# A hybrid decoder layer on one core: 512-column output projection, spread tables, shared gate-weight buffers, division on ScalarE, odd quarters' low parts on VectorE

## The chip, the cores and the metric

The kernel runs on one core of one Trainium2 chip. A core has TensorE (PE, the matrix unit), VectorE (DVE), ScalarE (ACT), GpSimd (POOL) and SyncE (SP), which here issues the DMAs. Each engine works through its own list of instructions in order and waits on semaphores for the others. The metric is the device time of one execution in microseconds (us); lower is better.

## The reference

The input is x (2048 positions by 1024) and 256 memory rows. All is float32.

```python
hn = _rmsnorm(h, norm_g[l])
proj = hn @ w_in[l]
(a_in, a_gate, c_in, c_b, c_c, c_gate, q, q_gate) = jnp.split(proj, split_idx, axis=-1)
y_ssm = _s5_group(a_in, ...) * jax.nn.silu(a_gate)
y_conv = _short_conv_group(c_in, c_b, c_c, conv_w[l], conv_b[l]) * jax.nn.silu(c_gate)
y_mem = _memory_xattn_group(q, mem_n, w_mem_kv[l]) * jax.nn.silu(q_gate)
```

The widths are 384 for each of the six state-space and convolution parts and 256 for q and its gate. The state-space group (`_s5_group`) is a scan over positions, a GELU, and a sigmoid gate with a 384 by 384 weight `w_glu`. The memory group is a softmax attention of four heads over the 256 memory rows. The three outputs are concatenated (1024 wide), multiplied by `w_out` (1024 by 1024), added to the residual x, and normalised once more.

## The kernel before

**Tiling.** The 2048 positions are worked in four quarters of 512 (q = 0 to 3). Every float32 product is made of three TensorE matmuls (`mm3`, L79 to L83): each operand is split into a rounded "high" part and the rest, the "low" part, and high times high, high times low and low times high are added up in PSUM. `split` (L85) makes the high part by a copy on ScalarE (L86) and the low part by a subtraction on VectorE or GpSimd (L77).

**Weights.** `wtile` (L127) loads 512 KB of weights into a staging buffer (two of them for most weights), splits it, and keeps both parts in one of three shared buffers (tag "wl"). Its argument `e` is the engine of the low part: in `proj` that is VectorE for quarter 0 and GpSimd for quarters 1 to 3. An odd quarter has 22 such tiles (3 for a_in, 2 for q, 2 for its gate, 3 for the a-gate, 12 for the convolution). The weights of the output projection (`wout`, tag names wo) have eight tiles per quarter, each 512 rows by 256 columns. The GLU's weights (`wg`) have three tiles of 128 columns with buffers of their own ("wg"), staged in a buffer that the loads of the scan's outputs (`gr`) use too.

**Stages.** In order of time: a prologue with the first rows and the projection of a_in for quarter 0; the gate and attention projections of quarter 0 with the building of four tables of the scan (`gen_table`) woven in at a fixed rate by `interleave`; the convolution of quarter 0, keys and values of the memory; then for quarters 1 and 3 the projections (`main`, all of 512 columns) together with the scan over two quarters (`ssm`, tiles W, sC, ps_y, ps_v), the GLU (`glu`, psg) and the attention (`attention`: scores sps, exponential pe, transposes trp, product po); quarter 2 with less beside it; and after each a stage of output projection (`outproj`, matmuls of 256 columns into PSUM tiles po). The last stage is `outproj(3)` with the GLU of quarter 2 woven in, then `outproj_last(2)`.

**What sets the order.** The Tile framework schedules the program with its own timeline and writes a fixed list for each engine, so a change in one part can move instructions elsewhere. PSUM banks and buffers are reused in a ring: a matmul into a new tile waits until the reader of the tile that held the bank before has finished. `gate2` (L619: ua, uq, uc) is such a reader: it frees the bank of a projection.

**The division.** In `attention` the 128 by 256 pieces of exponentials are divided by their sums on VectorE (L785); 64 such instructions in all.

Of the kernel before, what the change touches and what calls it, by code (L numbers as in the profile page):

```python
# [15 lines left out]
P = 128  # L16
# [29 lines left out]
def hymba_layer_kernel(  # L46
# [29 lines left out]
    def tt(o, a, b, op, e=V):  # L76
        e.tensor_tensor(o, a, b, op)  # L77
# [22 lines left out]
    def sumsq(xt, ss, junk):  # L100
        S.activation(junk, xt, AF.Square, accum_out=ss)
# [586 lines left out]
    def merge(a, b, rate):  # L688

# [70 lines left out]
    def attention(q, j):  # L760
# [52 lines left out]
    def glu(q):  # L813
# [13 lines left out]
            split(y_ssm[:, 0, t], y_ssm[:, 1, t], gr)  # L827
            yield
        for m in range(3):
            w = wtile(w_glu[0, :, m * P:(m + 1) * P], WS, P, f"wg{q}{m}", V, late["wg"], "a")  # L830
            ps = ps_ss.tile([P, QL], F32, tag="ss", name=f"psg{q}{m}")
            for k in range(3):
                mm3(ps, w[:, 0, k, :], w[:, 1, k, :], y_ssm[:, 0, k, :], y_ssm[:, 1, k, :], k == 0, k == 2)
            t_, g2 = (swk.tile([P, QL], F32, tag="pg", bufs=2, name=f"gt{q}{m}{z}") for z in range(2))
            S.activation(t_, ps, AF.Tanh, bias=bg[:, m:m + 1], scale=0.25)
            tt(g2, f32(y_ssm[:, 0, m, :]), f32(y_ssm[:, 1, m, :]), ALU.add, G)
            V.scalar_tensor_tensor(g2, t_, 1.0, g2, ALU.add, ALU.mult)
            V.scalar_tensor_tensor(us[m], g2, 0.125, us[m], ALU.mult, ALU.mult)
            yield
# [2 lines left out]
        yield  # L842


    yk = [("ssm", 0), ("ssm", 1), ("ssm", 2), ("conv", 0), ("conv", 1), ("mem", 0), ("mem", 1), ("conv", 2)]
    rows = [0, 1, 2, 3, 4, 6, 7, 5]

    def fetch_y(q):

# [16 lines left out]
    def omm(q, ps, i, kh, w, first):  # L866

        o_ = slice(i * P, (i + 1) * P)
        for k in range(4):
            nm, kk = yk[4 * kh + k]  # L870
            kr = rows[4 * kh + k] - 4 * kh
            mm3(ps, Y[q][nm][:, 0, kk, o_], Y[q][nm][:, 1, kk, o_], w[:, 0, kr, :], w[:, 1, kr, :],
                first and k == 0, kh == 1 and k == 3, skip_group_check=True)

    def residual(q, last=False):

# [9 lines left out]
                nc.sync.dma_start(h[z][u * NCH:(u + 1) * NCH], xq[q, u][:, 2 * z:2 * z + 2])  # L886
        return h

    def wout(q, n_, kh, dst=None, st="w", e=G):
        src = w_out[0, kh * 512:(kh + 1) * 512, n_ * 256:(n_ + 1) * 256]  # L890
        return wtile(src, 512, 256, f"wo{q}{n_}{kh}", e, dst, st)

    def outproj(q):
        h = residual(q)
        for n_ in range(4):
            ns = slice(n_ * 256, (n_ + 1) * 256)
            pss = [ps_mm.tile([P, 2, 256], F32, tag="mm", name=f"po{q}{n_}{b}") for b in range(2)]
            for kh in range(2):
                w = wout(q, n_, kh)
                for i in range(4):  # L900
                    omm(q, pss[i // 2][:, i % 2, :], i, kh, w, kh == 0 and i % 2 == 0)
                    yield
            for b in range(2):
                hb = h[b][:, :, ns]
                tt(hb, pss[b], hb, ALU.add)
# [15 lines left out]
    def outproj_last(q):  # L921
# [14 lines left out]
        ws = [[wout(q, n_, kh, dsts[2 * n_ + kh], "wx"[kh], V if kh else G) for kh in range(2)] for n_ in range(4)]  # L936
# [11 lines left out]
        for n_ in range(4):  # L948
            ns = slice(n_ * 256, (n_ + 1) * 256)
            ps = ps_mm.tile([P, 2, 256], F32, tag="mm", name=f"po{q}{n_}")  # L950
            for kh in range(2):
                for i in range(2):
                    omm(q, ps[:, i, :], i, kh, ws[n_][kh], kh == 0 and i == 0)
            for i in range(2):
                tt(h[i][:, ns], ps[:, i], h[i][:, ns], ALU.add)
                sumsq(h[i][:, ns], ss[:, i, n_:n_ + 1], junk[0][:, 0:256])
        for i in range(2):
            V.scalar_tensor_tensor(h[i], h[i], rstd(i, 4), fg_b, ALU.mult, ALU.mult)
            store(i, h[i])
        for i in range(2, 4):  # L960
            parts = [(0, 1), (2, 3)] if i == 2 else [(0, 1), (2,), (3,)]
            for b, ns_ in enumerate(parts):
                ns = slice(ns_[0] * 256, ns_[-1] * 256 + 256)
                ps = ps_mm.tile([P, 2, 256], F32, tag="mm", name=f"po{q}{i}_{b}")
                for a, n_ in enumerate(ns_):
                    for kh in range(2):
                        omm(q, ps[:, a, :], i, kh, ws[n_][kh], kh == 0 and a == 0)
                pv = ps.rearrange("p a n -> p (a n)")[:, :256 * len(ns_)]
                tt(h[i][:, ns], pv, h[i][:, ns], ALU.add)
                sumsq(h[i][:, ns], ss[:, i, b:b + 1], junk[1][:, :256 * len(ns_)])  # L970
# [35 lines left out]
    kv = memory_kv()  # L1006
# [49 lines left out]
```

## Time and profile before

| | before |
|---|---|
| median of three runs | 902.94 us (900.92 to 909.04) |
| the profiled execution | 904.45 us |
| its span from first to last instruction | 902.5 us |
| PE busy | 843.1 us (93%) |
| PEld (loading of weights into the array, beside PE) | 723.7 us (80%) |
| DVE busy | 613.7 us (68%) |
| ACT busy | 367.0 us (41%) |
| POOL busy | 301.7 us (33%) |
| mean granted TensorE clock | 0.975 |

A busy share counts instructions that overlap only once; TensorE's matmuls are pipelined, so the duration of one is longer than the distance to the next. Idle time of an engine is shown with what released it. "Granted clock" is the share of TensorE's full clock that the chip allowed in a stretch.

### The profile page before, as it was taken

The numbers are of one execution on the slowest core, as the hardware profiler recorded it, in microseconds if no ns is written. First come the engines' busy times: TensorE is split into PE (matmuls) and PEld (weight loads), VectorE is DVE, ScalarE is ACT, GpSimd is POOL, SyncE is SP. The second block draws the span as 40 slices with busy tenths as digits, with TensorE's granted clock in tenths as the row PEclk, the third lists the DMA queues.
The fourth block names the chain that finished last, engine by engine and source line by source line (L and its number), as shares of the span: only waits on it lengthen the run. The fifth ranks groups of instructions, "written<-read, shape, count | busy, mean of one in ns | idle before, by whom it ended". The sixth has DMA issues, their size and how long they took to land. (4 is left out here: it accounts for less than half of the span.)

```text
span 902.5 us, 13173 instructions
## 1 busy us (share of the span) xinstructions
PE 843.1 (93%) x4876; PEld 723.7 (80%) x4876; DVE 613.7 (68%) x1244; ACT 367.0 (41%) x706; POOL 301.7 (33%) x157
## 2 busy tenths in 40 slices
PE   2998999889998998999999899999999998989996
PEld 2985777778877877899888688899878876879996
DVE  6898899583998896936434664344399996865353
ACT  5343433545343434433444533335233344444511
POOL 2000001154222344444545434334443343455400
PEclk9999899999997999999999999999999999999999
DMA  9553649966464534454575632656757744493362
GB/s 205 161 150 103 189 131 269 267 187 201 125 179 130 156 93 119 108 152 141 159 239 150 160 114 84 161 165 186 214 156 207 211 128 125 117 222 112 125 177 57
DMA packets 180647, 142.97 MB, mean 158 GB/s; under 512 B 41192, under 2 KB 164584, under 8 KB 180584
## 3 DMA queue, kind: packets, MB, share of 16 engines
q1 hardware_dynamic: 180584, 142.14, 56.4%
q8 instruction: 38, 0.62, 0.3%
q14 instruction: 25, 0.20, 0.1%
HBM read 113.80 MB, written 26.74 MB: 156 GB/s over the span
## 5 line engine op out<-in xcount | busy, mean ns | idle before, releaser
L77 POOL TENSOR_TENSOR wo<-wo_st,wo 128x1024 fp32r<-128x1024 f32 x26 | 63.8, 2454 | 70.6 <-ACT wo L86 59.2
L77 DVE TENSOR_TENSOR h<-po,h 128x512 f32<-128x512 f32 (+1 forms) x37 | 22.2, 615 | 43.5 <-PE po L83 34.5
L81 PE MATMUL po<-wo,yssm 128*128 128x256 f32 x168 | 48.5, 289 | 1.8 <-ACT yssm L86 1.8
L83 PE MATMUL po<-wo,yssm 128*128 128x256 f32 x168 | 48.2, 287 | 0.0
L82 PE MATMUL po<-wo,yssm 128*128 128x256 f32 x168 | 47.8, 285 | 0.0
L780 ACT ACTIVATE pe<-sps,nm 128x256 f32<-128x256 f32 x64 | 29.5, 472 | 39.4 <-DVE nm L778 35.1
L81 PE MATMUL psai<-hn,wai 128*128 128x512 f32 (+1 forms) x120 | 42.7, 362 | 2.8 <-ACT hn L86 2.1
L82 PE MATMUL psai<-hn,wai 128*128 128x512 f32 (+1 forms) x120 | 42.5, 356 | 0.3 <-DVE hn L77 0.2
L83 PE MATMUL psai<-hn,wai 128*128 128x512 f32 (+1 forms) x120 | 42.0, 353 | 0.0
L81 PE MATMUL pscg<-hn,wcg 128*128 128x512 f32 x96 | 39.8, 415 | 2.2 <-ACT wcg L86 2.2
L86 ACT CAST wo<-wo_st 128x1024 fp32r<-128x1024 f32 x27 | 28.2, 1044 | 33.3 <-PE po L83 16.2
L81 PE MATMUL po<-wo,yconv 128*128 128x256 f32 x144 | 40.7, 283 | 0.0
L83 PE MATMUL po<-wo,yconv 128*128 128x256 f32 x144 | 40.3, 280 | 0.0
L82 PE MATMUL po<-wo,yconv 128*128 128x256 f32 x144 | 40.1, 279 | 0.0
L83 PE MATMUL pscg<-hn,wcg 128*128 128x512 f32 x96 | 39.1, 407 | 0.5 <-DVE wcg L77 0.5
L81 PE MATMUL psag<-hn,wag 128*128 128x512 f32 x96 | 39.5, 411 | 0.0
L82 PE MATMUL pscg<-hn,wcg 128*128 128x512 f32 x96 | 39.0, 407 | 0.0
L77 POOL TENSOR_TENSOR wcb<-wcb_st,wcb 128x1024 fp32r<-128x1024 f32 x9 | 22.9, 2550 | 47.9 <-ACT wcb L86 47.9
L83 PE MATMUL psag<-hn,wag 128*128 128x512 f32 x96 | 38.5, 401 | 0.0
L82 PE MATMUL psag<-hn,wag 128*128 128x512 f32 x96 | 38.4, 400 | 0.0
L81 PE MATMUL pscb<-hn,wcb 128*128 128x512 f32 x96 | 38.3, 399 | 0.0
L81 PE MATMUL psci<-hn,wci 128*128 128x512 f32 x96 | 38.3, 399 | 0.0
(710 smaller groups left out, 2903.5 us busy)
## 6 DMA issues: line engine op xcount, KB each, us to landing
wo_st<-in_w_out_dram SPq DMA_DIRECT2D x32, 512.0 KB, 3.8
tb<-t_dram SPq DMA_DIRECT2D x16, 960.0 KB, 5.5
out_dram<-h SPq DMA_DIRECT2D x32, 256.0 KB, 3.4
h<-in_x_dram SPq DMA_DIRECT2D x14, 512.0 KB, 7.4
wai_st<-in_w_in_dram SPq DMA_DIRECT2D x12, 512.0 KB, 4.3
wag_st<-in_w_in_dram SPq DMA_DIRECT2D x12, 512.0 KB, 4.3
wci_st<-in_w_in_dram SPq DMA_DIRECT2D x12, 512.0 KB, 4.2
wcc_st<-in_w_in_dram SPq DMA_DIRECT2D x12, 512.0 KB, 4.1
```

What stands on the lines that cost most here:

```text
L77: e.tensor_tensor(o, a, b, op)
L81: T.matmul(ps, lh, rh, start=first, stop=False, **kw)
L82: T.matmul(ps, lh, rl, start=False, stop=False, **kw)
L83: T.matmul(ps, ll, rh, start=False, stop=last, **kw)
L86: S.copy(hi, src)
L780: S.activation(pe[:, a, h], sps[h][:, a], AF.Exp, bias=nm_[:, a, h:h + 1], accum_out=sm[:, a, h:h + 1])
```

## The change

Five things are edited. (1) The output projection uses matmuls of 512 columns: a tile of weights is now 256 rows by 512 columns, and four PSUM banks (three "mm", one "po") are filled over four pairs of row blocks. Only the last 512 columns of the last 128 rows are done as two matmul groups of 256, so 1,488 of the 1,536 matmuls of 256 columns become 744 of 512 and 48 stay. (2) The tables of the scan are woven in at a lower rate and over a longer stretch, up to the keys and values of the memory. (3) The GLU's weights are two tiles (256 and 128 columns) in the shared "wl" and "ws" buffers. (4) The division by the softmax's sums moves from VectorE to ScalarE. (5) The low parts of the projections' weights for quarters 1 and 3 move from GpSimd to VectorE.

```diff
     def proj(q, c0, nm):
-        w = wtile(w_in[0, :, c0:c0 + P], DM, P, f"w{nm}{q}", G if q else V)
+        w = wtile(w_in[0, :, c0:c0 + P], DM, P, f"w{nm}{q}", G if q == 2 else V)
...
+    def weave(main, side, rate):
+        acc = 0.0
+        for _ in main:
+            acc += rate
+            while acc >= 1.0:
+                acc -= 1.0
+                next(side, None)
+            yield
...
             for a in range(2):
                 for h in range(2):
-                    V.tensor_scalar(pe[:, a, h], pe[:, a, h], sm[:, a, h:h + 1], None, ALU.mult)
+                    S.activation(pe[:, a, h], pe[:, a, h], AF.Copy, scale=sm[:, a, h:h + 1])
...
         for m in range(3):
-            w = wtile(w_glu[0, :, m * P:(m + 1) * P], WS, P, f"wg{q}{m}", V, late["wg"], "a")
+            if m % 2 == 0:
+                c1 = min(m * P + 256, WS)
+                wg = wtile(w_glu[0, :, m * P:c1], WS, c1 - m * P, f"wg{q}{m}", V)
+            w = wg[:, :, :, m % 2 * P:m % 2 * P + P]
...
+    def omm(q, ps, i, kp, w, cs=slice(0, 512)):
         o_ = slice(i * P, (i + 1) * P)
+        for k in range(2):
+            nm, kk = yk[2 * kp + k]
+            mm3(ps, Y[q][nm][:, 0, kk, o_], Y[q][nm][:, 1, kk, o_], w[:, 0, k, cs], w[:, 1, k, cs],
+                kp == pairs[0] and k == 0, kp == pairs[-1] and k == 1)
...
+    def wout(q, nh, kp, dst=None, st="w", e=G):
+        src = w_out[0, kp * 256:(kp + 1) * 256, nh * 512:(nh + 1) * 512]
+        return wtile(src, 256, 512, f"wo{q}{nh}{kp}", e, dst, st)
...
-        for n_ in range(4):
-            ns = slice(n_ * 256, (n_ + 1) * 256)
-            pss = [ps_mm.tile([P, 2, 256], F32, tag="mm", name=f"po{q}{n_}{b}") for b in range(2)]
-            for kh in range(2):
-                w = wout(q, n_, kh)
+        for nh in range(2):
+            ns = slice(nh * 512, (nh + 1) * 512)
+            pss = [ps_mm.tile([P, 512], F32, tag="mm", name=f"po{q}{nh}{b}") for b in range(3)]
+            pss.append(ps_po.tile([P, QL], F32, tag="po", name=f"po{q}{nh}3"))
+            for kp in pairs:
+                w = wout(q, nh, kp)
                 for i in range(4):
-                    omm(q, pss[i // 2][:, i % 2, :], i, kh, w, kh == 0 and i % 2 == 0)
+                    omm(q, pss[i], i, kp, w)
                     yield
...
-    interleave(chain(agate(0), qproj(0), conv(0, 0), conv(0, 1)), chain(mem_rows(), gens), 2.2)
+    side = chain(mem_rows(), gens)
+    for _ in weave(chain(agate(0), qproj(0), conv(0, 0), conv(0, 1)), side, 1.5):
+        pass
+    interleave(weave(merge(conv(0, 2), memory_kv(), 0.7), side, 0.9), prep(1), 2.0, 4)
+    for _ in side:
+        pass
     open_left()
-    interleave(merge(conv(0, 2), kv, 0.7), prep(1), 2.0, 4)
```

The first place is VectorE in the fourth block of the first scan (about 272 to 279 us before). sC is the scan's state that the ps_y matmuls read; uq (L619) is the reader that frees the PSUM bank which the third a-gate projection of quarter 1 (psag) takes next. Before, from the one to the other:

```order
482 L77 TENSOR_TENSOR sC_2799<-W_2793,m203w 128x3x128
483 L809 SCALAR_TENSOR_TENSOR uq_1190<-pe_2124,uq_1190 128x512
484 L539 COPY st_2421<-sC_2799 128x3
485 L523 STREAM_SHUFFLE m_2906<-ps_v_2810 128x384
486 L77 TENSOR_TENSOR m_2906<-m_2906,tb_2808 128x384
487 L535 COPY sC_3017<-st_137 128x3
488 L77 TENSOR_TENSOR m_2905<-ps_v_2810,tb_2808 128x384
489 L77 TENSOR_TENSOR m_2905<-m_2905,m_2906 128x384
490 L619 SCALAR_TENSOR_TENSOR uq_2633<-thq_2631,psqg_2606 128x512
```

In the changed kernel sC_2796 is row 488, and these are the last twelve rows to the same uq; the eight rows between are two score maxima, parts of the attention's output and the first steps of the next scan block:

```order
497 L552 SCALAR_TENSOR_TENSOR m103g<-m103g,ps_y_2854 128x384
498 L77 TENSOR_TENSOR m_2903<-m_2903,tb_2805 128x384
499 L77 TENSOR_TENSOR m_2902<-m_2902,m_2903 128x384
500 L792 RECIPROCAL sm_2503<-sm_2503 128x4
501 L530 SCALAR_TENSOR_TENSOR W_2908<-rho,st_138,m_2902 128x128 x3
502 L788 TENSOR_REDUCE nm_2646<-sps_2632 128x2
503 L554 SCALAR_TENSOR_TENSOR ge_2862<-m103g,ps_y_2854 128x384
504 L533 STREAM_SHUFFLE m204w<-W_2908 128x384
505 L788 TENSOR_REDUCE nm_2646<-sps_2633 128x2
506 L77 TENSOR_TENSOR W_2908<-W_2908,tb_2805 128x384
507 L77 TENSOR_TENSOR m204w<-m204w,tb_2805 128x384
508 L619 SCALAR_TENSOR_TENSOR uq_2630<-thq_2628,psqg_2603 128x512
```

The reader moved from 8 rows behind sC to 20 rows behind it.

The second place is ScalarE at the start of the stage of `outproj(3)`. thc is the last step on the last projection of quarter 3, hy are high parts of quarter 2's outputs, wo are output weights, wg the GLU's weights. Before:

```order
458 L617 ACTIVATE thc_7300<-pscg_7275 128x512
459 L86 CAST hy_7307<-fy_7308 128x512 x2
460 L86 CAST hy_7307<-fy_7314 128x512 x2
461 L86 CAST hy_7307<-fy_7320 128x512
462 L86 CAST wo_7531<-wo_st 128x1024
463 L86 CAST ymem_6906<-uq_6265 128x512
464 L86 CAST yconv_6506<-uc_7302 128x512
465 L86 CAST wg_7405<-wg_st 128x384
```

And in the changed kernel:

```order
468 L86 CAST wg_6981<-wg_st 128x768
469 L86 CAST yssm_6521<-ua_6011 128x512
470 L813 COPY pe_5786<-po_6813 64x2x256
471 L86 CAST yssm_6521<-ua_6078 128x512
472 L86 CAST ymem_6509<-uq_5868 128x512
473 L617 ACTIVATE thc_6898<-pscg_6873 128x512
474 L86 CAST hy_6905<-fy_6906 128x512 x2
475 L86 CAST hy_6905<-fy_6912 128x512 x2
476 L86 CAST hy_6905<-fy_6918 128x512
477 L86 CAST wo_7002<-wo_st 128x1024
```

The cast of the first GLU weights moved from seven rows behind thc to five rows ahead of it; the second tile of output weights (wo_7002) stands behind thc and the hy casts.

The third place is GpSimd between the memory's values (wv) and the first output weights (wo). Before, the list begins so, and goes on with the other low parts of quarter 1's weights:

```order
24 L77 TENSOR_TENSOR wv_1961<-wv_st,wv_1961 128x1024
25 L77 TENSOR_TENSOR wai_2093<-wai_st,wai_2093 128x1024
26 L77 TENSOR_TENSOR wai_2155<-wai_st,wai_2155 128x1024
27 L77 TENSOR_TENSOR wai_2225<-wai_st,wai_2225 128x1024
28 L77 TENSOR_TENSOR wq_2390<-wq_st,wq_2390 128x1024
```

In the changed kernel the whole stretch up to the output weights is this:

```order
23 L77 TENSOR_TENSOR wv_1888<-wv_st,wv_1888 128x1024
24 L77 TENSOR_TENSOR q13r<-q13v,mhalf 128x1
25 L77 TENSOR_TENSOR ymem_3062<-uq_2557,ymem_3062 128x512
26 L77 TENSOR_TENSOR yconv_2869<-uc_3105,yconv_2869 128x512
27 L77 TENSOR_TENSOR q20r<-q20v,mhalf 128x1
28 L77 TENSOR_TENSOR yconv_2869<-uc_3394,yconv_2869 128x512
29 L77 TENSOR_TENSOR q21r<-q21v,mhalf 128x1
30 L77 TENSOR_TENSOR gt_3429<-yssm_3348 128x512
31 L77 TENSOR_TENSOR gt_3477<-yssm_3348 128x512
32 L77 TENSOR_TENSOR gt_3498<-yssm_3348 128x512
33 L77 TENSOR_TENSOR wo_3664<-wo_st,wo_3664 128x1024
```

No weight's low part is left there on GpSimd; the 22 of them stand in VectorE's list.

## Rows read from the trace of the kernel before

**Rows 1.** The head of the page: span, then busy time of each engine.
```profile
span 902.5 us, 13173 instructions
PE 843.1 (93%) x4876; PEld 723.7 (80%) x4876; DVE 613.7 (68%) x1244; ACT 367.0 (41%) x706; POOL 301.7 (33%) x157
```

**Rows 2.** Windows by stage: stretch, its length, busy us (instructions) per engine, clock, DMA.
```profile
43.00:100.00 57.00, 51.66 (x245) 39.61 (x244) 49.25 (x152) 23.46 (x47) 1.10 (x2) 0.91 0.55 143
160.00:217.00 57.00, 51.85 (x291) 43.88 (x290) 33.88 (x67) 29.55 (x66) 23.59 (x12) 0.97 0.82 229
217.00:381.00 164.00, 155.75 (x796) 128.51 (x795) 141.65 (x267) 71.02 (x145) 56.99 (x27) 0.97 0.45 131
381.00:433.00 52.00, 50.18 (x415) 49.68 (x414) 26.59 (x38) 19.69 (x35) 22.00 (x11) 0.97 0.53 145
433.00:578.00 145.00, 141.40 (x654) 114.85 (x653) 72.45 (x116) 62.07 (x119) 65.44 (x31) 0.98 0.51 149
626.00:791.00 165.00, 158.57 (x801) 130.90 (x800) 129.90 (x232) 66.41 (x128) 64.54 (x29) 0.99 0.58 162
791.00:893.00 102.00, 98.01 (x791) 95.63 (x790) 51.24 (x80) 37.91 (x75) 38.69 (x21) 0.98 0.54 148
```

**Rows 3.** Groups of the page: output projection (256 columns) and a-gate projection (512).
```profile
L81 PE MATMUL po<-wo,yconv 128*128 128x256 f32 x144 | 40.7, 283 | 0.0
L81 PE MATMUL psag<-hn,wag 128*128 128x512 f32 x96 | 39.5, 411 | 0.0
```

**Rows 4.** Timeline of PE, 256 columns: first and last of 35 in a row.
```profile
399.93 0.28 PE L81 MATMUL po<-wo,yssm 128*128 128x256 f32 x1
...
403.90 0.28 PE L82 MATMUL po<-wo,yconv 128*128 128x256 f32 x1
```

**Rows 5.** Timeline of PE, 512 columns: first and last of 23 in a row.
```profile
487.75 0.39 PE L82 MATMUL psag<-hn,wag 128*128 128x512 f32 x1
...
492.74 0.39 PE L83 MATMUL psag<-hn,wag 128*128 128x512 f32 x1
```

**Rows 6.** Waits of PE: for whom, total us, times, longest.
```profile
PE ps_y L548 <- DVE sC L77: 9.9, 6, 3.1
PE psg L81 <- ACT wg L86: 8.0, 4, 3.4
PE trq L144 <- DVE hn L77: 4.1, 2, 2.8
PE psqg L81 <- DVE uq L619: 4.1, 1, 4.1
```

**Rows 7.** Groups of low parts of weights: GpSimd, then VectorE in quarter 0.
```profile
L77 POOL TENSOR_TENSOR wcb<-wcb_st,wcb 128x1024 fp32r<-128x1024 f32 x9 | 22.9, 2550 | 47.9 <-ACT wcb L86 47.9
...
L77 DVE TENSOR_TENSOR wcb<-wcb_st,wcb 128x1024 fp32r<-128x1024 f32 x3 | 3.7, 1217 | 5.1 <-ACT wcb L86 5.1
```

**Rows 8.** Groups of VectorE with one shape, 128 by 1.
```profile
L77 DVE TENSOR_TENSOR ssq<-ssq 128x1 f32<-128x1 f32 x16 | 2.4, 156 | 21.5 <-ACT junkq L101 21.5
L77 DVE TENSOR_TENSOR q22a<-q22r 128x1 f32<-128x1 f32 x1 | 2.4, 2396 | 0.7 <-POOL q22r L77 0.7
```

**Rows 9.** The division's line (min/median/max ns), its group, and ScalarE's exponential of one shape.
```profile
L785 DVE TENSOR_SCALAR pe<-pe,sm x64: 341/349/2544, 206.6 to 769.6; 128x256 f32<-128x256 f32 x64
...
L785 DVE TENSOR_SCALAR pe<-pe,sm 128x256 f32<-128x256 f32 x64 | 29.4, 524 | 0.2
...
L780 ACT ACTIVATE pe<-sps,nm 128x256 f32<-128x256 f32 x64 | 29.5, 472 | 39.4 <-DVE nm L778 35.1
```

**Rows 10.** Timelines of VectorE and of PE in the fourth scan block of quarter 1.
```profile
272.39 2.38 DVE L77 TENSOR_TENSOR sC<-W,m203w 128x384 f32<-128x384 f32 x1
...
278.50 0.68 DVE L619 SCALAR_TENSOR_TENSOR uq<-thq,psqg 128x512 f32<-128x512 f32 x1
...
274.82 0.80 PE L548 MATMUL ps_y<-sC,tb 128*128 128x128 f32 x2 [3.12 <-DVE sC L77]
...
279.43 0.79 PE L81 MATMUL psag<-hn,wag 128*128 128x512 f32 x1
```

**Rows 11.** Timelines of PE, SP and ScalarE at the start of `outproj(3)`.
```profile
802.49 0.50 PE L81 MATMUL psg<-yssm,wg 128*128 128x512 f32 x1 [3.40 <-ACT wg L86]
...
799.53 4.23 SPq L131 DMA_DIRECT2D wg_st<-in_w_glu_dram  x2
...
801.92 0.51 ACT L86 CAST wg<-wg_st 128x384 fp32r<-128x384 f32 x1 [4.44 <-DMA wg_st<-in_w_glu_dram]
```

More of the change, by code (lines that the diff above doesn't have):

```diff
@@ L842, in glu @@
         yield
-    yk = [("ssm", 0), ("ssm", 1), ("ssm", 2), ("conv", 0), ("conv", 1), ("mem", 0), ("mem", 1), ("conv", 2)]
-    rows = [0, 1, 2, 3, 4, 6, 7, 5]
+    yk = [("ssm", 0), ("ssm", 1), ("ssm", 2), ("conv", 0), ("conv", 1), ("conv", 2), ("mem", 0), ("mem", 1)]
+    pairs = (0, 1, 3, 2)
     def fetch_y(q):
@@ L864, in fetch_y @@
                 split(t[:, 0], t[:, 1], st[:, k], V if k else G)
-    def omm(q, ps, i, kh, w, first):
+    def omm(q, ps, i, kp, w, cs=slice(0, 512)):
         o_ = slice(i * P, (i + 1) * P)
[L869 to L873, printed above, removed]
+        for k in range(2):
+            nm, kk = yk[2 * kp + k]
+            mm3(ps, Y[q][nm][:, 0, kk, o_], Y[q][nm][:, 1, kk, o_], w[:, 0, k, cs], w[:, 1, k, cs],
+                kp == pairs[0] and k == 0, kp == pairs[-1] and k == 1)
     def residual(q, last=False):
@@ L887, in residual @@
         return h
-    def wout(q, n_, kh, dst=None, st="w", e=G):
-        src = w_out[0, kh * 512:(kh + 1) * 512, n_ * 256:(n_ + 1) * 256]
-        return wtile(src, 512, 256, f"wo{q}{n_}{kh}", e, dst, st)
+    def wout(q, nh, kp, dst=None, st="w", e=G):
+        src = w_out[0, kp * 256:(kp + 1) * 256, nh * 512:(nh + 1) * 512]
+        return wtile(src, 256, 512, f"wo{q}{nh}{kp}", e, dst, st)
     def outproj(q):
         h = residual(q)
-        for n_ in range(4):
-            ns = slice(n_ * 256, (n_ + 1) * 256)
-            pss = [ps_mm.tile([P, 2, 256], F32, tag="mm", name=f"po{q}{n_}{b}") for b in range(2)]
-            for kh in range(2):
-                w = wout(q, n_, kh)
+        for nh in range(2):
[4 more added lines that the diff above has]
+                w = wout(q, nh, kp)
                 for i in range(4):
-                    omm(q, pss[i // 2][:, i % 2, :], i, kh, w, kh == 0 and i % 2 == 0)
+                    omm(q, pss[i], i, kp, w)
                     yield
-            for b in range(2):
-                hb = h[b][:, :, ns]
-                tt(hb, pss[b], hb, ALU.add)
+            for i in range(4):
+                hb = h[i // 2][:, i % 2, ns]
+                tt(hb, pss[i], hb, ALU.add)
         jk = tmp.tile([P, QL], F32, tag="ci", name=f"junk{q}")
@@ L928, in wv_ @@
         def wv_(t):
-            return t[:, :2 * 4 * 256].rearrange("p (z k n) -> p z k n", z=2, k=4)
-        dsts = [None, None, None, Y[q]["rest"].rearrange("p z a (b n) -> p z (a b) n", b=2)]
-        dsts.append(wv_(kvp.tile([P, 2 * 4 * 256], F32R, tag="vd", name="wvd")))
+            return t[:, :2 * 2 * 512].rearrange("p (z k n) -> p z k n", z=2, k=2)
+        dsts = [None, None, None, Y[q]["rest"]]
+        dsts.append(wv_(kvp.tile([P, 2 * 2 * 512], F32R, tag="vd", name="wvd")))
         dsts.append(wv_(stab.tile([P, GB * TW], F32, tag="tb", name="wtb").bitcast(F32R)))
@@ L935, in outproj_last @@
         dsts.append(wv_(late["ym"].tile([P, 2 * 2 * QL], F32R, tag="ym", name="wym")))
-        ws = [[wout(q, n_, kh, dsts[2 * n_ + kh], "wx"[kh], V if kh else G) for kh in range(2)] for n_ in range(4)]
+        ws = [{kp: wout(q, nh, kp, dsts[4 * nh + a], "wx"[a % 2], V if a % 2 else G) for a, kp in enumerate(pairs)}
+              for nh in range(2)]
         ss, jk = (sml.tile([P, 4, 4], F32, tag=t_, bufs=1, name=t_) for t_ in ("ssl", "ssk"))
@@ L947, in outproj_last @@
         junk = [tmp.tile([P, QL], F32, tag=t_, name="junk" + t_) for t_ in ("ci", "u")]
[L948 to L951, printed above, removed]
+        for nh in range(2):
+            ns = slice(nh * 512, (nh + 1) * 512)
+            pss = [ps_mm.tile([P, 512], F32, tag="mm", name=f"po{q}{nh}{i}") for i in range(2)]
+            for kp in pairs:
                 for i in range(2):
-                    omm(q, ps[:, i, :], i, kh, ws[n_][kh], kh == 0 and i == 0)
+                    omm(q, pss[i], i, kp, ws[nh][kp])
@@ L954, in outproj_last @@
             for i in range(2):
-                tt(h[i][:, ns], ps[:, i], h[i][:, ns], ALU.add)
-                sumsq(h[i][:, ns], ss[:, i, n_:n_ + 1], junk[0][:, 0:256])
+                tt(h[i][:, ns], pss[i], h[i][:, ns], ALU.add)
+                sumsq(h[i][:, ns], ss[:, i, nh:nh + 1], junk[0])
         for i in range(2):
-            V.scalar_tensor_tensor(h[i], h[i], rstd(i, 4), fg_b, ALU.mult, ALU.mult)
+            V.scalar_tensor_tensor(h[i], h[i], rstd(i, 2), fg_b, ALU.mult, ALU.mult)
@@ L959, in outproj_last @@
             store(i, h[i])
         for i in range(2, 4):
[L961 to L970, printed above, removed]
+            parts = [(0, 512), (512, 1024)] if i == 2 else [(0, 512), (512, 768), (768, 1024)]
@@ L971, in outproj_last @@
+            for b, (c0, c1) in enumerate(parts):
+                ns = slice(c0, c1)
+                ps = ps_mm.tile([P, 512], F32, tag="mm", name=f"po{q}{i}_{b}")[:, :c1 - c0]
+                for kp in pairs:
+                    omm(q, ps, i, kp, ws[c0 // 512][kp], slice(c0 % 512, c0 % 512 + c1 - c0))
+                tt(h[i][:, ns], ps, h[i][:, ns], ALU.add)
+                sumsq(h[i][:, ns], ss[:, i, b:b + 1], junk[1][:, :c1 - c0])
                 tt(hg[:, i - 2, ns], h[i][:, ns], fg_b[:, ns], ALU.mult)
@@ L983, in open_left @@
         phs.close()
-        for n_ in ("yc", "ym", "wg"):
+        for n_ in ("yc", "ym"):
             late[n_] = ctx.enter_context(tc.tile_pool(name=n_, bufs=1, reuse_waits="tile"))
@@ L1005, in hymba_layer_kernel @@
     gens = chain(*[z for b in range(NB) for z in (gen_table(b), gen_turns(2 * b), gen_turns(2 * b + 1))])
-    kv = memory_kv()
-    interleave(chain(agate(0), qproj(0), conv(0, 0), conv(0, 1)), chain(mem_rows(), gens), 2.2)
+    side = chain(mem_rows(), gens)
[4 more added lines that the diff above has]
+        pass
     open_left()
-    interleave(merge(conv(0, 2), kv, 0.7), prep(1), 2.0, 4)
     interleave(ain(1), chain(attention(0, 0), attention(0, 1)), 2.5)
```

## Prediction, written before the changed kernel was run

> **What bounds the kernel now.** I read the head of the page first [rows 1]: TensorE is busy 843.1 of 902.5 us, VectorE 613.7, the others under half. So time is saved in two ways only: less work on TensorE, or fewer gaps in it. The windows by stage show the gaps [rows 2]: length less PE's busy time is 5.3, 5.2, 8.3, 1.8, 3.6, 6.4 and 4.0 us, together 34.6. A second loss stands in their clock column: one minus the granted clock, times the length, gives 5.1, 1.7, 4.9, 1.6, 2.9, 1.7 and 2.0 us, together 19.9. So about 54 us can be had from waits at the very most; the rest is TensorE's own pace. The reader is to see how full VectorE is in two of these stages: 141.65 of 164 us beside the first scan, 129.90 of 165 beside the second, but 72.45 of 145 in quarter 2, where there is no scan.
>
> Who is waited for stands in PE's waits [rows 6]: the scan's state sC (9.9 us in six waits), the GLU's weights wg (8.0 in four), hn (4.1), and one bank of the gate projection (4.1). The first two are what the change can reach.
>
> **512 columns.** The groups of the page suggest a trap [rows 3]: 283 ns for a matmul of 256 columns, 411 for one of 512. By these, 1,488 x 0.283 - 744 x 0.411 would save 115 us. But matmuls overlap, and what costs time is the distance between starts: 34 steps of 256 columns take 403.90 - 399.93 = 3.97 us, 0.1168 each [rows 4]; 22 steps of 512 take 4.99 us, 0.2268 each [rows 5]. A pair saves 2 x 0.1168 - 0.2268 = 0.0068 us, and 744 pairs save 5.1 us, with 0 and 9 as bounds (the single steps of 256 columns that the timeline prints are 0.11 to 0.12). **Term: -5.**
>
> **Low parts on VectorE.** Each odd quarter moves 22 tiles from 2.55 us on GpSimd to 1.22 us on VectorE [rows 7]; quarter 0 already does this. VectorE gains 22 x 1.22 = 26.8 us of work per odd quarter, some 17 tiles or 20.7 us of it beside the scan. Against it stands what GpSimd now costs VectorE: a 128 by 1 operation takes 0.156 us as a rule, and 2.396 us where it starts beside GpSimd's subtraction [rows 8]; the division's median is 349 ns, its mean 524, its longest 2,544 [rows 9]; sC took 2.38 us [rows 10]. With GpSimd's weights gone from these stages (third place in the order) most of that should go. Its size isn't in one row: it lies between 0 and 17 x 2.5 = 42 us per stage, and I take about half of 42, 21 us, since only operations that happen to start beside a subtraction are stretched. So this edit leaves VectorE's amount of work as it is, and makes its single steps shorter and less uneven.
>
> **Division on ScalarE.** VectorE loses 64 x 0.524 = 33.5 us by the group's mean (29.4 busy), and ScalarE gains 64 x 0.472 = 30.2 by the nearest row, the exponential of the same shape [rows 9]. ScalarE is busy 71 of 164 us in the fuller stage [rows 2], so it has the room. The price is a longer chain: ScalarE's list now waits for the reciprocal, and behind it stand the high parts of weights and the tanh of the gates. I take 0 for it; 64 waits of half a microsecond that nobody hides would be 32 us, which is the far bound.
>
> **What that does to the waits for sC.** The longest, 3.12 us [rows 10], was sC itself at 2.38 us with two readers of the attention ahead of it. In the new order sC stands ahead of those, but behind a low part of 1.22 us. I take half of the 9.9 us [rows 6] away, between none and all. **Term: -5.**
>
> **The GLU's weights.** Four waits, 8.0 us. The worst is at the start of the last stage [rows 11]: SyncE issued these weights only at 799.53, behind other loads, ScalarE had them at 801.92, PE went on at 802.49. In the new order their cast stands ahead of the last projection's tanh (second place), and PE does 18 matmuls of 512 columns before it needs them, 18 x 0.227 = 4.1 us. The second scan's GLU is likewise entered earlier. I take 6 of the 8.0 away, between 0 and 8. **Term: -6.** What is late next is the second tile of output weights, wo_7002: its cast is behind tanh and five hy casts, its low part behind GpSimd's; PE has 24 output matmuls and 18 of the GLU ahead of it, 42 x 0.227 = 9.5 us. I allow a new wait of 1 us, between 0 and 3. **Term: +1.**
>
> **A bank that comes free later.** The first place in the order speaks against the change. Before, the reader uq ended 278.50 + 0.68 = 279.2, and psag started 279.43, right behind the scores of the attention [rows 10]. Now 20 rows lie between sC and the end of uq instead of 8. From the end of sC (274.8) to that of uq were 4.4 us with 8 rows; 20 such rows are 11 us. PE's work in between stays what it was, 279.43 - 274.82 = 4.6 us. So PE would stand 6 us, between 0 and 9, before psag. **Term: +6.**
>
> **Other edits.** The slower tables leave the first projections' waits nearly as they are: the bank that costs 4.1 us [rows 6] is freed by an operation that stays behind one that waits for DMAs. VectorE's shorter steps should ease a few of the small waits for hn, pT and wcg that make up the rest of the 34.6 us: **term -1.5**, between -6 and +4.
>
> The waits together: -5 - 6 + 1 + 6 - 1.5 = -5.5 us of 34.6, or 16%. The clock falls behind such gaps (0.91 and 0.97 in stages with them, 0.98 and 0.99 where they are fewer [rows 2]), so I take a part of 16% of the 19.9 us: **term -2.5**.
>
> Sum: -5 - 5.5 - 2.5 = **-13 us**. The profiled execution took 904.45 us, 1.5 above the median of 902.94 and inside the runs' spread; 904.45 - 13 is 891.5, and from the median it is 890. I predict **890 us**.
>
> **Rivals.**
>
> *Stalls only move.* The waits that go (sC, wg) come back as others (the bank of psag, wo_7002, casts behind divisions), and only the 512 columns remain: 903 - 5 = 898 us, within 1%. For it speaks that the framework makes the whole order anew, and that I found one new long wait by reading few places. Chance 0.27.
>
> *Nearly all waits go.* Without GpSimd's interference VectorE is early everywhere: -5, -9.9, -8, bank +2, other waits -4, and of the clock -6: -31 us, 872 us. Against it: VectorE's amount of work hardly falls. Chance 0.14.
>
> *VectorE becomes the bound.* It is slower if the stretching isn't GpSimd's weights. Then in the first scan's stage VectorE has 141.65 + 20.7 less the 7 us that the division there costs at its undisturbed price, and waits for late weights: in quarter 0 it stood idle 5.1 us before three tiles [rows 7]; one such wait per odd quarter makes 160 of 164 us. An engine so full, with PE waiting for each step, can't keep PE fed: if it needs the same slack as now (141.65 of 164, 86%), the stage grows to 160 / 0.86 = 186, 22 us more. With the second scan's stage at 129.90 + 20.7 - 5 + 5 = 151 of 165, or 175 at 86%, 10 more, less the 5 of the columns: 930 us; half of it is 916. It decides once VectorE's work beside the first scan rises over about 150 us. Against it: the 2.396 us of an operation of 0.156 [rows 8] can hardly be its own. Chance 0.12 (912 and above).
>
> *Weight loads are the pace.* At 256 columns the loads fill the stage of output projection (49.68 of 52 us), less so in projections of 512 (128.51 of 164) [rows 2]. If the load alone set the pace, half as many would save 744 x 0.1168 = 87 us: 816. The step of 0.2268 at 512 columns with a load each [rows 5] speaks flatly against it. Chance 0.02. The Trainium skill's page "TensorE: Matmul & The Clock Gate", section "Back-to-back issue gap", gives 131 ns per matmul of 512 columns sustained, and by that estimate the saving would be 744 x (0.2336 - 0.131) = 76 us. The trace doesn't agree: 227 ns, near the page's isolated gap of 512 / 2.4 + 2.5 = 216.
>
> **How the numbers follow.** The forecast's own case (880 to 897) has the remaining 0.45. The range must leave out at most 2 in 10: down to 874 it takes in part of the good case, up to 909 all of the case in which stalls only move and none of the slow one. A difference of 1% (9 us) is about what a measurement of this kernel can tell from none, its three runs being 8 us apart. Faster by over 1% is below 893.9: two thirds and more of the forecast's case (0.35), the good case (0.14), the loads (0.02) and a little of the stalls that move (0.04): 0.55. Slower by over 1% is above 912: 0.12, and 0.01 from the rest. Within: 0.32.
>
> **What would show it.** The new profile should have PE starts 0.227 apart in the output projection; 128 by 1 operations of VectorE at 0.16 us throughout the odd quarters; about 27 us of weights' low parts on VectorE per odd quarter and GpSimd nearly idle there; ps_y's wait for sC at about 5 us; psg's wait for wg at about 2; a wait of psag for uq of about 6 us with a lower clock behind it; VectorE's busy time beside the scans no higher than now. I am wrong if VectorE's busy time there rises, if casts on ScalarE wait for the division's reciprocals and PE for them, or if SyncE's order makes other weights late.

## The result and the profile after

| | before | changed |
|---|---|---|
| median | 903.68 us (four runs, 900.92 to 909.04) | 892.29 us (four runs, 889.80 to 893.49) |
| ratio, 95% interval | 1 | 0.9863 [0.9831, 0.9896] |
| span of the profiled execution | 902.5 us | 891.7 us |
| PE busy | 843.1 us | 834.0 us |
| GpSimd busy | 301.7 us | 194.3 us |
| waits of PE for sC | 9.9 us | 0.3 us |

The change gains 1.4%, near the forecast of 890 us, and its interval leaves out a ratio of 1. But the sum hides large terms of both signs, as the parts below show.

The head of the changed kernel's page answers to [rows 1]:

```profile
span 891.7 us, 11628 instructions
PE 834.0 (94%) x4132; PEld 685.9 (77%) x4132; DVE 595.1 (67%) x1216; ACT 391.2 (44%) x758; POOL 194.3 (22%) x113
```

Weight loads fell with the number of matmuls, VectorE lost 18.6 us of busy time, ScalarE took on 24.2, and GpSimd lost a third of its work.

The windows by stage of the changed kernel, cut where its own stages begin and end, answer to [rows 2] (the columns are the same):

```profile
44.00:100.00 56.00, 51.17 (x243) 39.32 (x243) 48.38 (x151) 23.69 (x47) 1.10 (x2) 0.94 0.55 145
160.00:223.00 63.00, 53.26 (x303) 44.82 (x302) 34.67 (x70) 29.16 (x60) 10.60 (x6) 0.92 0.83 222
223.00:385.00 162.00, 155.53 (x802) 129.03 (x801) 131.60 (x265) 84.40 (x181) 14.65 (x10) 0.97 0.46 138
385.00:433.00 48.00, 47.93 (x225) 39.16 (x224) 22.80 (x35) 20.86 (x38) 22.23 (x11) 1.00 0.64 167
433.00:577.00 144.00, 140.40 (x652) 114.03 (x651) 70.39 (x99) 66.39 (x130) 65.22 (x31) 0.99 0.51 149
625.00:782.00 157.00, 155.54 (x794) 129.22 (x793) 121.72 (x235) 72.44 (x140) 12.88 (x8) 1.00 0.58 166
782.00:883.00 101.00, 95.71 (x437) 78.02 (x435) 56.71 (x76) 35.50 (x64) 41.00 (x22) 1.00 0.54 152
```

Worked as in the prediction, PE's gaps are 4.8, 9.7, 6.5, 0.1, 3.6, 1.5 and 5.3 us, together 31.5 where there were 34.6; the clock's part is 14.7 where it was 19.9. The second scan's stage (625 to 782) has almost no gap left, the stretch around the memory's keys and values (160 to 223) has nearly twice as much as before.

PE's waits behind the prologue answer to [rows 6] (for whom, us in total, times, longest). No wait for wg is left, 0.3 us are left for sC, and others stand at the head of the list:

```profile
PE psqg L81 <- DVE uq L619: 4.5, 1, 4.5
...
PE psv L82 <- POOL wv L77: 3.4, 1, 3.4
PE trq L144 <- DVE xb L602: 3.3, 1, 3.3
PE po L82 <- POOL wo L77: 3.0, 3, 1.2
PE sps L783 <- ACT pe L790: 3.0, 1, 3.0
PE ps_v L511 <- DMA tb<-t_dram: 2.9, 1, 2.9
PE po L81 <- DVE h L77: 2.3, 1, 2.3
...
PE ps_v L511 <- DVE sC L77: 0.3, 1, 0.3
```

### The profile page after: what moved, and what is told of

Read it like the earlier page. It is cut to its first block, busy times and chain, and to the rows that moved or that the text cites. A ratio compares the mean times of both kernels' runs of the same rounds, so it can differ in the third digit from the quotient of the medians.

```text
span 891.7 us, 11628 instructions
## 1 busy us (share of the span) xinstructions
PE 834.0 (94%) x4132; PEld 685.9 (77%) x4132; DVE 595.1 (67%) x1216; ACT 391.2 (44%) x758; POOL 194.3 (22%) x113
## 5 line engine op out<-in xcount | busy, mean ns | idle before, releaser
L77 POOL TENSOR_TENSOR wo<-wo_st,wo 128x1024 fp32r<-128x1024 f32 x26 | 66.1, 2541 | 51.8 <-ACT wo L86 50.0
L81 PE MATMUL pscg<-hn,wcg 128*128 128x512 f32 x96 | 38.7, 403 | 0.0
L83 PE MATMUL pscb<-hn,wcb 128*128 128x512 f32 x96 | 37.7, 392 | 0.9 <-DVE wcb L77 0.9
L81 PE MATMUL psci<-hn,wci 128*128 128x512 f32 x96 | 38.4, 400 | 0.0
L82 PE MATMUL pscg<-hn,wcg 128*128 128x512 f32 x96 | 38.3, 399 | 0.0
L81 PE MATMUL pscb<-hn,wcb 128*128 128x512 f32 x96 | 38.2, 398 | 0.0
L83 PE MATMUL pscg<-hn,wcg 128*128 128x512 f32 x96 | 38.2, 397 | 0.0
L81 PE MATMUL pscc<-hn,wcc 128*128 128x512 f32 x96 | 38.1, 397 | 0.0
L83 PE MATMUL pscc<-hn,wcc 128*128 128x512 f32 x96 | 37.7, 393 | 0.3 <-DVE wcc L77 0.3
L83 PE MATMUL psci<-hn,wci 128*128 128x512 f32 x96 | 37.8, 394 | 0.0
L82 PE MATMUL psci<-hn,wci 128*128 128x512 f32 x96 | 37.6, 391 | 0.0
L82 PE MATMUL pscc<-hn,wcc 128*128 128x512 f32 x96 | 37.5, 391 | 0.0
L77 POOL TENSOR_TENSOR ymem<-uq,ymem 128x512 fp32r<-128x512 f32 x4 | 5.2, 1296 | 148.3 <-DMA wcg_st<-in_w_in_dram 132.9
L82 PE MATMUL pscb<-hn,wcb 128*128 128x512 f32 x96 | 37.5, 391 | 0.0
L77 DVE TENSOR_TENSOR hn<-trq,hn 128x512 fp32r<-128x512 f32 x32 | 21.4, 683 | 23.3 <-ACT hn L86 23.3
```

The costliest lines, as they stand in the source:

```text
L81: T.matmul(ps, lh, rh, start=first, stop=False, **kw)
L82: T.matmul(ps, lh, rl, start=False, stop=False, **kw)
L83: T.matmul(ps, ll, rh, start=False, stop=last, **kw)
```

## The experiments

All ratios are to the kernel before, timed beside it on the same chip. The table gives stage lengths in us, from the first start of PE in one stage to the first in the next, of one profiled execution each, which lies up to 4.2 us from its kernel's median. One execution differs from the next: "columns alone" and "columns, other order" have the same lists on VectorE, ScalarE and GpSimd up to 392 us, yet their "tables, kv" took 100.0 and 95.6 us. "Tables, kv" runs from the first convolution of quarter 0 to the a_in projection of quarter 1; "scan 1" and "scan 2" are the stages of quarters 1 and 3; "out 1" is quarter 1's output projection and "out 0" quarter 0's; "end" is quarter 3's and 2's together, up to PE's last start.

| kernel | tables, kv | scan 1 | out 1 | quarter 2 | out 0 | scan 2 | end | ratio, interval |
|---|---|---|---|---|---|---|---|---|
| before | 99.0 | 164.2 | 52.2 | 145.0 | 48.3 | 164.8 | 102.4 | 1 |
| changed | 104.4 | 160.8 | 48.1 | 144.2 | 48.0 | 157.7 | 100.6 | 0.9863 [0.9831, 0.9896] |
| columns alone | 100.0 | 163.5 | 48.9 | 145.1 | 48.1 | 162.9 | 99.4 | 0.9907 [0.9880, 0.9935] |
| columns, other order | 95.6 | 166.5 | 48.3 | 144.0 | 48.2 | 164.6 | 98.7 | 0.9942 [0.9920, 0.9964] |
| low parts alone | 97.8 | 157.7 | 57.1 | 145.6 | 48.3 | 167.2 | 104.4 | 1.0008 [0.9990, 1.0026] |
| division alone | 98.5 | 157.6 | 49.5 | 143.9 | 48.4 | 164.6 | 106.2 | 0.9962 [0.9940, 0.9985] |
| GLU weights alone | 99.1 | 166.7 | 51.3 | 142.3 | 49.4 | 163.8 | 101.1 | 1.0011 [0.9984, 1.0038] |
| low parts and GLU weights | 97.3 | 156.6 | 50.4 | 142.3 | 48.4 | 158.7 | 108.0 | 0.9886 [0.9866, 0.9907] |
| changed, low parts back | 105.7 | 162.4 | 50.3 | 145.1 | 48.1 | 166.5 | 101.9 | 1.0088 [1.0067, 1.0108] |
| changed, idle subtractions | 103.9 | 173.5 | 48.1 | 144.0 | 48.1 | 167.1 | 106.5 | 1.0196 [1.0158, 1.0233] |
| changed, tables back | 97.3 | 159.9 | 47.8 | 144.2 | 48.1 | 156.6 | 102.1 | 0.9801 [0.9774, 0.9827] |
| and a gate buffer | 99.2 | 150.6 | 48.0 | 144.0 | 48.1 | 157.2 | 101.6 | 0.9698 [0.9665, 0.9731] |
| tables back, quarter 2 on VectorE | 96.9 | 160.3 | 48.1 | 139.4 | 48.2 | 156.7 | 102.4 | 0.9762 [0.9726, 0.9797] |
| all three | 97.1 | 150.6 | 48.0 | 139.6 | 48.1 | 157.5 | 103.5 | 0.9651 [0.9622, 0.9681] |

### Each part alone

Four kernels, each the kernel before with one part of the diff. The columns:

> The kernel before with the 512-column output projection alone. By the prediction's term (0.0068 us per pair of matmuls) it gains 5 us, ratio 0.9945, and TensorE starts 0.227 us apart in the output projection. Rival: the changed kernel's trace has stages of output projection of 48.1 us without a gap where the kernel before has 48.3, so the columns give 1 us or less and the ratio is 0.998 to 1.000; what they do then is to take the weight loads' busy time down (49.7 to about 39 us per stage), not the time.

Measured: 0.9907, a gain of 8.4 us, more than either theory. The stage that never had a gap ("out 0") says what the pace gives: 48.3 to 48.1 us, while the busy time of the weight loads there fell from 47.9 to 39.1 us, as the rival said. So the term's reason is wrong although its size is near: the gain stands in stages that had waits (out 1, scan 2, end).

The low parts:

```diff
-        w = wtile(..., f"w{nm}{q}", G if q else V)
+        w = wtile(..., f"w{nm}{q}", G if q == 2 else V)
```

> The kernel before with only the odd quarters' low parts moved to VectorE. Theory: GpSimd's subtractions stretched VectorE's operations beside the scans, so the two stages of quarters 1 and 3 lose 3 us and 7 us as in the changed kernel: ratio 0.988 to 0.992, PE's waits for sC go from 9.9 us to under 3. Rival (VectorE is too full, the gain is the division's): 1.000 or slower, waits for sC stay.

Measured: 1.0008. The theory's mechanism is there: no wait for sC stands among PE's waits any more, and scan 1 lost 6.5 us. But the gain was lost again in the output stages, 4.9 in "out 1" and 2.0 in "end", and scan 2 grew. PE's waits of this kernel, from the list by line, show on whom:

```profile
PE po L81 <- ACT yssm L86: 6.7, 3, 4.6
...
PE psg L83 <- DVE wg L77: 4.4, 1, 4.4
...
PE psg L81 <- ACT wg L86: 3.5, 2, 2.2
```

These are the GLU's weights and its outputs. That a slow scan had covered them before is a reading of this list; the next part tests it.

The division:

> The kernel before with only the division moved to ScalarE. Theory: it relieves VectorE by 29 us but no wait of PE names it, so the ratio is 0.997 to 1.000. Rival: the gain beside the scans is the division's: 0.990 to 0.993.

Measured: 0.9962, a little below the theory's range, its whole interval on the side of a gain. Scan 1 lost 6.6 us, "end" grew by 3.8 at a granted clock of 0.95 (0.98 before); why it fell there no run shows.

The GLU's weights:

> The kernel before with only the GLU's weights in two tiles of the shared buffers. By the prediction's term, PE's 8.0 us of waits for wg fall to about 2 and the ratio is 0.993. Rival: the weights are staged in the same two buffers as all others and make those late, the ratio is 0.998 to 1.005.

Measured: 1.0011. The wait for wg went as foretold (none is left in the list of PE's waits), and others of the same size took its place, as the rival said.

```profile
PE po L799 <- DVE pT L77: 6.5, 5, 2.3
PE po L81 <- DVE h L77: 4.8, 3, 2.1
...
PE pscc L81 <- ACT wcc L86: 2.5, 1, 2.5
```

### Do two parts need each other?

> The kernel before with two edits together: odd quarters' low parts on VectorE and the GLU's weights in the shared buffers, each of which alone gave nothing (1.0008 and 1.0011). Theory: the low parts take the scan's waits away, and the gain was lost again because the GLU's weights came late from their staging buffer, which the scan's outputs share; with both, the stages of quarters 1 and 3 keep the 6 us each and the ratio is 0.988 to 0.992. Rival, that edits simply add: 1.000 to 1.004.

Measured: 0.9886. Neither edit gives anything alone; together they give 10 us. Scan 1 is 7.6 us shorter, scan 2 6.1. The rival, that the edits add, falls. (In "end" 5.6 us are lost again, to a wait of 4.1 us for the low part of yssm among others, and the clock there is 0.95.)

> The changed kernel with the odd quarters' low parts back on GpSimd. Theory (low parts count in company): 0.993 to 0.998, 6 to 10 us slower than the changed kernel, PE's waits for sC back at 6 us or more. Rival (low parts are worth nothing): 0.986, as the changed kernel.

Measured: 1.0088, outside both expectations: 20 us slower than the changed kernel, and slower than the kernel before. Without this edit the whole gain is gone. The window of scan 1 in this kernel, cut where its own stage begins and ends, is:

```profile
229.00:391.00 162.00, 154.11 (x794) 126.06 (x794) 137.04 (x247) 80.68 (x170) 56.73 (x28) 0.98 0.44 130
```

VectorE's 247 instructions take 0.55 us each here, against 131.60 / 265 = 0.50 in the changed kernel's scan 1, although the low parts of 1.22 us are no longer among them. But the 20 us are not the price of the stretching alone. PE's waits for sC come back with 4.4 us only, less than expected; scan 1 grows by 1.6 us and scan 2 by 8.8; and the framework's lists are new (106 of VectorE's 1,172 instructions stand in another order). By what the runs here give for each of the other four edits (8.4 and 3.4 gained, nothing, 5.6 lost to the tables) this kernel should be 6 us faster than the one before, and it is 8 us slower: those 14 us stand between the edits, and no run parts them.

### Is it the interference itself?

In the changed kernel each projection weight of quarters 1 and 3 gets two subtractions on GpSimd, into a scratch tile that nobody reads:

```diff
+        if q % 2:
+            scr = late["scr"].tile([P, QL], F32, tag="scr", name=f"scr{nm}{q}")
+            hi = f32(w[:, 0].rearrange("p k n -> p (k n)"))
+            for z in range(2):
+                tt(scr, hi[:, z * QL:(z + 1) * QL], hi[:, z * QL:(z + 1) * QL], ALU.subtract, G)
```

> The changed kernel plus two subtractions of 128x512 on GpSimd for each projection weight of quarters 1 and 3, whose result nobody reads (about 2.6 us per weight, as much as the low part took there). Theory (GpSimd's subtractions reading SBUF stretch VectorE's operations, and that alone cost the time): VectorE's busy time beside the scans rises by 15 us or more per stage with the same instructions, the waits come back, ratio 1.000 to 1.020. Rival (the gain came from the low parts being ready 1.3 us earlier, or from the new order): 0.985 to 0.990, as the changed kernel.

Measured: 1.0196, 30 us slower than the changed kernel, with the growth in scan 1 (12.7 us), scan 2 (9.4) and "end" (5.9, at a clock of 0.95 where the changed kernel had 1.00), and none in quarter 2 or in the two output projections ahead of it and behind it. Its windows of scan 1 and scan 2, cut at its own stages:

```profile
225.00:399.00 174.00, 156.91 (x798) 128.16 (x797) 150.85 (x263) 83.07 (x177) 62.14 (x46) 0.96 0.43 127
639.00:806.00 167.00, 158.78 (x796) 130.57 (x795) 140.03 (x231) 69.78 (x137) 64.45 (x47) 0.99 0.53 154
```

In scan 1, 263 instructions of VectorE take 150.85 us (the changed kernel's 265 took 131.60), in scan 2, 231 take 140.03 (235 took 121.72): 18 to 19 us more per stage for nearly the same instructions. GpSimd's work, needed by nobody, makes VectorE slow and TensorE wait; the waits for sC come back with 4.1 us. The rival (low parts ready earlier, or a better order) can't give this: 1,182 of VectorE's 1,216 instructions stand in the same order as in the changed kernel. The idle subtractions also read the weights' buffer and could have held it from the next weights; the trace has one such wait, of 0.9 us:

```profile
ACT wci L86 <- POOL scrag L77: 0.9, 1, 0.9
```

It fits the Trainium skill, page "SBUF — State Buffer", section "Who interferes with whom", by which a VectorE instruction with two SBUF inputs contends with a GpSimd instruction that reads SBUF. The trace's 2.396 us for an operation of 0.156 [rows 8], beside a subtraction of the same length on GpSimd, is the size of it here.

### The columns' other half

```diff
-    pairs = (0, 1, 3, 2)
+    pairs = (1, 0, 3, 2)
```

> The kernel with the 512 columns alone (0.9907), but with the pairs of row blocks in the order 1, 0, 3, 2: the first weights now meet the third GLU output and the first convolution block, which are late. Theory: the columns themselves give 1 us, and the other 7 come from the finer tiles of two row blocks, by which the first 24 matmuls need only the two GLU outputs that are ready first; so the waits at the starts of the output stages come back and the ratio is 0.995 to 0.999. Rival (the columns' pace gives the 8 us): 0.991.

Measured: 0.9942 against 0.9907: 3.2 us, but the two intervals overlap, so the size is uncertain. The trace shows a wait of about that size. The kernel before waited 1.8 us for yssm early in quarter 1's output projection, the 512-column kernel not at all; with the other order a wait stands at its first matmul, by the timeline of PE:

```profile
381.82 0.70 PE L81 MATMUL po<-wo,yssm 128*128 128x512 f32 x1 [2.90 <-ACT yssm L86]
```

So tiles of two row blocks rather than four let the first matmuls need only the GLU outputs that are ready. With about 1 us of pace and 3 of order, some 4 us of the columns' 8.4 are left. Most of them stand in "end": the wait of 3.40 us for the GLU's weights at its start [rows 11] has gone in both kernels with 512 columns, though the code that loads these weights is the same. In the kernel with the columns alone this is left of it:

```profile
798.80 0.51 PE L81 MATMUL psg<-yssm,wg 128*128 128x512 f32 x1 [0.18 <-ACT wg L86]
...
800.50 0.50 PE L83 MATMUL psg<-yssm,wg 128*128 128x512 f32 x1 [0.50 <-DVE wg L77]
```

"End" is 3.0 us shorter here and 3.7 with the other order. Why the weights are early enough with the wider matmuls no run shows. So a part of the gain that the prediction gave to the GLU's own edit comes with the columns already.

### The tables

> The changed kernel with the tables woven in as before (all else changed). Theory: the stretch from the first convolution to the second quarter's projections grew from 99.0 to 104.4 us in the changed kernel because of the slower tables; back they give 5 us, ratio 0.980. Rival: the later tables free VectorE and SP's queue for the first scan, and that stage loses more than 5 us without them: 0.986 or above.

Measured: 0.9801, 5.6 us faster than the changed kernel: the slower tables are a loss, of the size that the stretch from 99.0 to 104.4 had shown. In that stretch of the changed kernel PE waits for wk (1.9 and 1.1 us), wv (3.4) and xb (3.3); with the tables back none of these waits is left, and 1.8 for wcg and 1.2 for hn stand there. How the tables make them is not shown. One candidate stands in the timelines of SP and ScalarE of the changed kernel:

```profile
160.56 4.44 SPq L434 DMA_DIRECT2D gt<-s_Kp  x6
165.10 0.54 SPq L131 DMA_DIRECT2D wk_st<-in_w_mem_kv_dram  x1
...
169.25 1.04 ACT L86 CAST wk<-wk_st 128x1024 fp32r<-128x1024 f32 x1 [0.98 <-DMA wk_st<-in_w_mem_kv_dram]
```

Six issues of a table stand in SP's list ahead of the memory's weights. But with the tables back, eight such issues stand ahead of them (8.74 us), and PE doesn't wait. Another candidate stands in the timeline of GpSimd: the second wv's low part took 3.97 us in the changed kernel, while VectorE built a table beside it, and both together 4.74 us with the tables back.

```profile
184.59 3.97 POOL L77 TENSOR_TENSOR wv<-wv_st,wv 128x1024 fp32r<-128x1024 f32 x1
...
184.20 4.74 POOL L77 TENSOR_TENSOR wv<-wv_st,wv 128x1024 fp32r<-128x1024 f32 x2 [0.46 <-ACT wv L86]
```

That would be 1.6 of the 3.4 us.

### The bank that comes free late

The kernel with the tables back, and a buffer of its own for the second attention gate of quarters 1 to 3:

```diff
-            yv["uq"].append(gate2(ps, f"uq{j}", f"q{q}{j}", 1, late["att"]))
+            yv["uq"].append(gate2(ps, f"uq{j}", f"q{q}{j}", 1, late["uqx" if q and j else "att"]))
```

> The kernel with the tables as before and all other edits (0.9801), with a buffer of its own for the second attention gate (uq) of quarters 1 to 3. Theory: the reader that frees psag's bank stands so late because its output buffer is still being stored for quarter 0 (VectorE stood 1.4 us for that transfer right before it); with its own buffer it moves ahead of sC, the 6 us in the first scan's fourth block go and the ratio is 0.972 to 0.976. Rival (VectorE's amount of work keeps it late): 0.979 to 0.981.

Measured: 0.9698 against 0.9801, 9.3 us faster than without it, and scan 1 is 9.3 us shorter. This is what the place looked like in the changed kernel (timelines of VectorE, SP and PE):

```profile
276.41 0.55 DVE L77 TENSOR_TENSOR sC<-W,m203w 128x384 f32<-128x384 f32 x1
...
288.08 0.69 DVE L619 SCALAR_TENSOR_TENSOR uq<-thq,psqg 128x512 f32<-128x512 f32 x1 [1.42 <-DMA y_dram<-uq]
...
280.31 0.33 SPq L630 DMA_DIRECT2D y_dram<-uq  x1
...
281.39 2.56 PE L783 MATMUL sps<-kd,qh 64*128 64x256 f32 x12 [2.99 <-ACT pe L790]
286.87 1.62 PE L511 MATMUL ps_v<-pg,tb 128*128 128x128 f32 x6 [2.92 <-DMA tb<-t_dram]
...
289.42 0.78 PE L81 MATMUL psag<-hn,wag 128*128 128x512 f32 x1
```

And with the buffer, the same operation of VectorE and the window of scan 1:

```profile
254.37 0.67 DVE L619 SCALAR_TENSOR_TENSOR uq<-thq,psqg 128x512 f32<-128x512 f32 x1
...
217.00:381.00 164.00, 164.00 (x858) 136.12 (x857) 134.26 (x268) 85.81 (x177) 20.66 (x13) 1.00 0.51 146
```

uq comes 36 us after the start of the stage's projections (218.7) instead of 64 (223.9), and PE has no gap at all in 164 us. The place had cost more than its 5.9 us of gaps: the clock of the window is 1.00 now. The kernel that differs by the buffer alone (tables back, 0.9801) had 5.9 us of gaps in its scan 1, too, and a clock of 0.97:

```profile
218.00:378.00 160.00, 154.08 (x797) 127.92 (x797) 131.53 (x263) 81.26 (x169) 14.59 (x10) 0.97 0.45 132
```

### Quarter 2, and all together

> The kernel with the tables as before and all other edits (0.9801), with the low parts of quarter 2 on VectorE too. Theory: quarter 2 has no scan, VectorE is half idle there and PE waits for it 4 us at most, so the gain is 0 to 3 us, ratio 0.977 to 0.980. Rival: VectorE's list delays the attention's transposes and it is slower, 0.982 or more.

Measured: 0.9762 against 0.9801, 3.5 us, a little over the range; the two intervals overlap. The stage of quarter 2 bears it out: it is 4.8 us shorter, and the waits there for the attention's transposes (pT, 3.5 and 1.9 us) are gone. Quarter 2 has no scan, yet it too had been slowed.

> The two last steps together: the gate's own buffer (0.9698 with the earlier tables) and quarter 2's low parts on VectorE (0.9762 against 0.9801, 4.1 us). They touch different stages, so the theory is that they add: 0.9698 - 0.0039 = 0.966, between 0.963 and 0.969. Rival: one moves the order of the other and the sum falls short, 0.970 or above.

Measured: 0.9651 [0.9622, 0.9681], 874.14 us (872.32 to 875.54): within the noise the two add (quarter 2 is 4.4 us shorter than with the gate's buffer alone), and this is the fastest of all kernels here, 19 us below the changed one by the ratios.

## Why the prediction was right, point by point

**What bounds the kernel.** Right: TensorE stayed the bound. Over the windows, 11 us shorter together, 3.1 us came from gaps and 5.2 from the clock; the rest is TensorE's own pace and the rounding of the windows.

**The sum.** That it came so near is partly luck. Three terms missed by 3 to 6 us in both directions and cancelled: the columns gave 8.4 for 5, the division 3.4 for 0, and the slower tables cost 5.6 for 0.

**512 columns, -5.** The size was near (8.4 alone), the reason wrong. The two pitches [rows 4, 5] were read from stretches of one kind each; in a stage where transposes come between, 192 matmuls of 512 columns took 48.0 us where 384 of 256 took 48.3. By the starts in the trace of "out 0", a step between two output matmuls is 0.233 us in the mean (median 0.229), and it was 0.118 for 256 columns: a pair saves 0.003 us, not 0.0068. The pace gave about 1 us over four stages. What the term left out is that a finer tile changes which outputs the first matmuls need, and that the wait for the GLU's weights in the last stage went with it.

**Low parts, and waits for sC, -5.** The mechanism was right and is shown by the idle subtractions; the size was too small. The waits for sC went from 9.9 to 0.3 us, and taking the edit out of the whole costs 20 us. That VectorE's busy time would not rise was right (131.6 beside the first scan, from 141.65). Not every small step became short: of the 128 by 1 operations, two took 1.2 us in the first scan.

**The division, 0.** Alone it gave 3.4 us. PE waited nowhere for ScalarE's division itself; the group of it in the changed kernel, by line, is steady where VectorE's was not [rows 9]:

```profile
L795 ACT ACTIVATE pe<-pe,sm x64: 492/495/529, 217.6 to 753.6; 128x256 f32<-128x256 f32 x64
```

**GLU weights, -6, and wo_7002, +1.** The 8.0 us of waits went altogether, and GpSimd's wo cost 3.0 in three waits: -5 in sum, as foretold. But alone the edit gave nothing; it was right only beside the low parts. And the columns alone took the waits for wg from 8.0 to 4.5 us, so the terms for the columns and for these weights overlap.

**The bank, +6.** The two gaps ahead of psag are 2.99 + 2.92 = 5.9 us, and psag starts 0.65 us after uq ends, as worked out from the order. The cause was only half read: VectorE's list explains a late uq, but the list was so because uq's buffer was still being stored. And the gaps inside carry other names (pe, tb), since PE's own list has those ahead of psag.

**Other edits, -1.5.** This step failed. I looked at the bank of the first projections, which indeed didn't move (4.1 and 4.5 us), and costed the slower tables at nothing. They cost 5.6 us around the memory's keys and values, where PE waited 9.7 us for wk, wv and xb; by which path is open. A wait for the evicted h at the change of column halves (2.3 us) was not in the sum either.

**The clock, -2.5.** It gave 5.2. The rule that it falls behind gaps fits only in part. Before, the second scan's stage had 6.4 us of gaps at 0.99, and quarter 1's output 1.8 at 0.97 [rows 2]; in the changed kernel the last stage's gaps grew from 4.0 to 5.3 us while its clock went from 0.98 to 1.00. Its cause stays open.

**Rivals.** "VectorE becomes the bound" fell with its condition; the weight loads as the pace fell with the stage of 48.0 us. "Stalls only move" was true of the low parts alone and of the GLU's weights alone, but not of the two together. "Nearly all waits go" (872 us) was not true of the change, whose gaps are 31.5 us of 34.6; only the last kernel, with two steps more and the tables back, comes to 874.

## What to carry to other kernels

An edit that gives nothing alone can be worth 1% beside another, because the wait it removes was covering the next one: test parts both alone and taken out of the whole. The cost of two engines that read the same memory side by side stood here in the durations of the one held up (0.16 us that becomes 2.4), not in its waits; a copy of the suspected work that nobody needs showed it in one run. When a reader frees a bank late, look at the buffer it writes to as well as at what stands ahead of it.

## What was unexpected of the hardware

The interference may go both ways: in one place of the changed kernel GpSimd's subtraction for the second wv took 3.97 us beside a busy VectorE, that for the first 2.40; no run tested it. A step of 512 columns in an output stage is a little longer than in a stretch of one kind: with the 32 transposes of "out 0" in between, at the 0.108 us that the same stage of the kernel before gives for each, (48.0 - 32 x 0.108) / 192 is 0.232 us against 0.2268.
